# Two-layer encoder: output weights on the sync queue behind two activation loads, and eight constant matmuls at the start

## The chip, the cores and the metric

The kernel runs on one core of a Trainium2 chip. A core has a matrix engine (TensorE, "PE" in the profile, with its weight loads listed as "PEld"), a vector engine (VectorE, "DVE"), a scalar engine (ScalarE, "ACT"), a general engine (GpSimd, "POOL") and a sync engine ("SP") that only issues transfers. Each engine runs its own instructions in their order and waits on semaphores for the others. Transfers between the main memory (HBM) and the on-chip memory (SBUF) are done by 16 DMA engines; in this kernel they are issued from SP and from POOL. Matmul results land in PSUM banks, which DVE and ACT read.

The metric is the device time of one execution in microseconds (us). Lower is better.

## The reference

A trunk of two layers over 1024 frames of width 1024, in float32. Layer 0 mixes with multi-head latent attention, layer 1 with differential attention; each mixer is followed by a residual and a LayerNorm, then by a SwiGLU block with a residual and a LayerNorm. What matters here is the start (the first projection of `x`) and the output projection of layer 1:

```python
h = x @ w_in                                   # layer 0, first work of the kernel
...
# layer 1, differential attention, 8 heads of 128 values
a = p[:, 0] - lam * p[:, 1]
o = jnp.einsum('bhqk,bkhe->bqhe', a, v)
o = _rmsnorm(o, g_sub) * (1.0 - lambda_init)
mix = o.reshape(b, s, DIFF_HEADS * DIFF_V) @ w_o
h = _layernorm(ALPHA * h + mix, g, b)
```

## The kernel before

**Products in parts.** Float32 operands are split into a high part and a remainder ("h" and "l"), and a product is three matmuls: high by high, high by low, low by high. ACT makes the high part, DVE or POOL the remainder.

**The planner.** The program is written in one order, and a planner with a timeline model then places each instruction in its engine's queue. Instructions stay in the order that the data need, but an instruction may be moved ahead of others that it does not depend on. Which DMA goes to which queue is fixed by the line that issues it (`nc.sync` is SP, `nc.gpsimd` is POOL); the place in the queue is the planner's.

**The start.** `load_x` and `load_w_in` (lines 930 to 952) bring the first two token blocks of `x` in quarters and the eight slices of the input weights, split them, and `project` (line 969) multiplies them. Line 979 and line 980 are its matmuls, for columns 0 to 383 and 384 to 703. Before the first of them the matrix engine has nothing to do. The tile `ones` (all entries 1/128) is filled by `V.memset` on line 1033; it is later the stationary side of the RMS norm in layer 1.

**The attention of layer 1.** The function `attention` (line 258) runs over 64 blocks: eight heads by eight token blocks of 128 rows. Head 7 takes its token blocks in the order `LAST_ORDER` = 6, 7, 4, 5, 2, 3, 0, 1. For a block, `score_b` makes two score maps (matmuls of line 216 into three "s" banks, biased and reduced by DVE on line 219, exponentials by ACT on line 222, POOL on line 1281, DVE on line 1282), `turn_b` transposes them (line 148), and `mix_b` multiplies with the values (line 255). Scores are made two blocks ahead. A list of fillers (`at(slot, ...)`) puts other work between the blocks.

**The output projection of layer 1** (class `OutProj`, line 325) is spread over the attention of head 7. At slot 54 `begin_out` (line 1369) closes the pool of the transposed activations and makes the object. Its constructor loads the activations of the first token block (`of`, six heads, 128 rows each of 512 B: line 354) from `o_dr`, where the attention has put the finished heads; then the output weights of the eight heads, already split, from `wo_dr` (1 MB a head). Heads 0 to 5 go to tiles of the pool `op1` (line 341); heads 6 and 7 go in halves to tiles of the pool `wp` (line 346). All ten weight loads are issued from POOL. `of` also splits the block (ACT on line 377, DVE on line 378) and loads its residual rows (line 372). For the second token block `of` is called by a filler four slots later. `early` multiplies heads 0 to 5 of the first and second token block (line 389) while head 7 is still under way: heads 0 and 1 of the first block at slot 56, heads 2 and 3 at slot 57, 4 and 5 at slot 58, then the second block at slots 60 and 61. `late` adds heads 6 and 7, which stay on the chip, and `rest` does the other six token blocks. In `rest` POOL also loads the gain and bias of the LayerNorm (line 419).

Of the kernel before, what the change touches and what calls it, by code (L numbers as in the profile page):

```python
# [16 lines left out]
P = 128  # L17
# [21 lines left out]
LAST_ORDER = (6, 7, 4, 5, 2, 3, 0, 1)  # L39
# [3 lines left out]
def trunk(  # L43
# [32 lines left out]
    nc = tc.nc  # L76
    V, A, G, T = nc.vector, nc.scalar, nc.gpsimd, nc.tensor
# [5 lines left out]
    ones = cp.tile([P, P], F32, tag="ones", name="ones")  # L83
# [15 lines left out]
    banks("ps0", PS_BUFS_A)  # L99
    dr = ctx.enter_context(tc.tile_pool(name="dr", bufs=1, space=DRAM))  # L100

    mhalf = cst[:, 0:2]
    V.memset(mhalf, -0.5)
    eps_rms = cst[:, 8:9]
# [2 lines left out]
    def f32(t):  # L107
        return t.bitcast(F32)
# [4 lines left out]
    def ps_s(name):  # L113
        return ps.tile([P, 512], F32, tag="s", bufs=ps_bufs[0], name=name)

    def ps_m(name):
        return ps.tile([P, 512], F32, tag="m", bufs=ps_bufs[1], name=name)
# [3 lines left out]

    def ps_o(name):
        return ps.tile([P, 512], F32, tag="o", bufs=ps_bufs[3], name=name) if len(ps_bufs) > 3 else ps_m(name)

    def small(name, n=1):
        return sp.tile([P, 2], F32, tag="small", name=name, bufs=22)[:, :n]
# [119 lines left out]
    def pv_group(pts, g, v_of, name):  # L246
        po = ps_o(f"o_{name}")
        nj = 2 * g + 2
        for j in range(nj):
            hi, lo = pts[j // 2]  # L250
            vh, vl = v_of(j)
            c = slice(P, 256) if j == nj - 1 else slice(0, 256)
            first, last = j == 0, j == nj - 1
            for a, b, st, sp_ in ((vh, hi, first, False), (vh, lo, False, False), (vl, hi, False, last)):
                T.matmul(po[:, c], a, b[:, j % 2, c], start=st, stop=sp_, skip_group_check=True)
        return po
# [68 lines left out]
    class OutProj:  # L325
# [5 lines left out]
        def __init__(self, side, w_dr, o_dram, o_here, x_src, x_dst, scale):  # L331
            self.st = ExitStack()
            self.pool = self.st.enter_context(tc.tile_pool(name="op1", bufs=2, side=side, reuse_waits="tile"))
            self.o_dram, self.o_here, self.x_src, self.x_dst, self.scale = o_dram, o_here, x_src, x_dst, scale
            self.oh, self.z, self.sums, self.m = {}, {}, {}, {}
            self.of(LAST_ORDER[0])
            self.wo = []
            for h in range(H):
                if h < self.HEADS:
                    t = self.pool.tile([P, 2, D], F32R, tag=f"wo{h}", name=f"wo1_{h}", bufs=1)  # L340
                    nc.gpsimd.dma_start(t, w_dr[h])
                    self.wo.append((t[:, 0], t[:, 1]))
                else:
                    t = [wp.tile([P, D], F32R, tag=f"w{p}", name=f"w{p}o1_{h}") for p in "hl"]
                    for p in range(2):
                        nc.gpsimd.dma_start(t[p], w_dr[h][:, p])
                    self.wo.append(t)

        def of(self, tb):
# [136 lines left out]
    def ffn(side, xo, xst, pending, layer, x_src, x_dst, lng, lnb, next_x):  # L486
# [419 lines left out]
        st.close()  # L906
        return new, rest, normed

    o_dr = [[dr.tile([H, P, 256], F32, name=f"o_dr{l}_{g}") for g in range(4)] for l in range(2)]
    wo_dr = [dr.tile([P, 2, D], F32, name=f"wo_dr{h}") for h in range(H)]  # L910
    xs_dr = [dr.tile([S, D], F32, name=f"xs_dr{l}") for l in range(3)]
# [118 lines left out]

    gs = cst[:, 16:17]
    nlam = cst[:, 24:25]
    V.memset(ones, 1.0 / P)
    lv = [late[:, 64 * i:64 * i + 64] for i in range(4)]
    dots = late[:, 256:258]

# [14 lines left out]
    with ast as st:  # L1051
# [100 lines left out]
        def at(slot, fn, *args):  # L1152
            fill.setdefault(slot, []).append(lambda: fn(*args))
# [49 lines left out]
    with ExitStack() as st:  # L1203
# [162 lines left out]
        first, second = LAST_ORDER[:2]  # L1366
# [7 lines left out]
        at(b, begin_out)  # L1374
        for slot, what, args in (
            (2, "early", (first, (0, 1))), (3, "early", (first, (2, 3))), (4, "early", (first, (4, 5))),
            (4, "of", (second,)), (6, "early", (second, (0, 1, 2))), (7, "early", (second, (3, 4, 5))),
            (9, "late", (first,)),
        ):
            at(b + slot, lambda what, *a: getattr(proj[0], what)(*a), what, *args)  # L1380
# [97 lines left out]
```

## Time and profile before

| | |
|---|---|
| median of 3 runs | 2318.11 us (2317.43 to 2320.41) |
| the profiled execution | 2317.24 us, of which its span is 2315.5 us |
| granted matrix clock over the span, mean | 0.992 |
| busy: PE, DVE, ACT, POOL | 2253.4, 1560.1, 1018.5, 891.9 us |
| DMA | 288.29 MB, 125 GB/s on average |

The span runs from the first to the last instruction of the profiled execution; the rest of its time lies around that. The matrix engine is busy for nearly all of the span, so the other engines' times matter only where the matrix engine waits for them. Busy shares are averages over stages with different limits; what an edit is worth is read at its own place.

### The profile page before, as it was taken

To read this page: it belongs to the slowest core of one execution; us is meant where nothing else is said; L and a number is where in the kernel's file an instruction comes from. 1 tells how busy PE (TensorE), PEld (TensorE's weight loads), DVE (VectorE), ACT (ScalarE), POOL (GpSimd) and SP (SyncE) were. 2 spreads that over 40 slices of the span, in tenths; PEclk is the share of its full clock that TensorE was granted. 3 is DMA by queue.
4 is the path that set the end of the run, shared out by engine and by line. 5 is a ranking of instruction groups with operands and counts; after the bars stand their busy time and mean duration, and the time that the engine had idled before them with its cause. 6 is when DMAs were issued, how large, how long until landed. Compare 5 with 4: busy or idle time off the path is not lost. (4 is left out here: it accounts for less than half of the span.)

```text
span 2315.5 us, 31126 instructions
## 1 busy us (share of the span) xinstructions
PE 2253.4 (97%) x11410; PEld 1918.7 (83%) x11410; DVE 1560.1 (67%) x2879; ACT 1018.5 (44%) x2092; POOL 891.9 (39%) x698
## 2 busy tenths in 40 slices
PE   9999999999999999999999999979999999999997
PEld 9898897888888887888888898967778888887886
DVE  5666664596666658677476766666596656658777
ACT  4466673352332324345465656545442333324343
POOL 2233351014444445465332423222014444436564
PEclk9999999999999999999999999989999999999999
DMA  5121335334323238454310202153344222337453
GB/s 202 41 91 69 106 101 178 125 142 145 125 76 129 86 119 322 182 183 140 101 46 31 71 25 69 37 191 111 126 144 149 99 103 102 113 129 303 146 203 121
DMA packets 103658, 288.29 MB, mean 125 GB/s; under 512 B 8528, under 2 KB 31696, under 8 KB 93008
## 3 DMA queue, kind: packets, MB, share of 16 engines
q1 hardware_dynamic: 98064, 268.46, 33.0%
q0 software_dynamic: 5440, 17.83, 2.3%
q8 instruction: 90, 1.47, 0.3%
q14 instruction: 64, 0.52, 0.1%
HBM read 205.00 MB, written 77.07 MB: 122 GB/s over the span
## 5 line engine op out<-in xcount | busy, mean ns | idle before, releaser
L469 ACT CAST op_g<-gr 128x512 fp32r<-128x512 f32 x240 | 147.5, 622 | 411.0 <-PE gb L514 228.3
L470 POOL TENSOR_TENSOR op_g<-gr,op_g 128x512 fp32r<-128x512 f32 x104 | 145.8, 1407 | 303.6 <-DVE tmp L605 153.6
L470 DVE TENSOR_TENSOR op_h<-rh,op_h 128x512 fp32r<-128x512 f32 x154 | 162.8, 1088 | 67.6 <-ACT op_h L469 67.6
L514 PE MATMUL ga<-xh_m,op_g 128*128 128x512 f32 x512 | 168.0, 389 | 0.0
L469 ACT CAST op_h<-rh 128x512 fp32r<-128x512 f32 x154 | 93.0, 619 | 145.0 <-PE dx L782 37.5
L782 PE MATMUL dw<-op_w_t,op_h 128*128 128x512 f32 x660 | 151.4, 390 | 0.0
L782 PEld LDWEIGHTS dw<-op_w_t,op_h 128*128 128x128 f32 x660 | 123.6, 188 | 25.9 <-DVE op_h L470 0.4
L222 ACT ACTIVATE l_b<-l_b,mx_b 128x256 f32<-128x256 f32 (+7 forms) x128 | 99.6, 778 | 76.2 <-DVE mx_b L219 74.2
L1281 POOL TENSOR_SCALAR l_b<-l_b,r_b,cst 128x128 f32<-128x128 f32 (+3 forms) x64 | 52.8, 825 | 205.1 <-DVE r_b L224 196.1
L470 POOL TENSOR_TENSOR op_w_t<-tt,op_w_t 128x512 fp32r<-128x512 f32 x66 | 98.8, 1501 | 77.1 <-ACT op_w_t L469 77.1
L782 PE MATMUL dx<-op_w_b,op_h 128*128 128x512 f32 x528 | 122.7, 392 | 5.9 <-ACT op_w_b L469 3.9
L782 PEld LDWEIGHTS dx<-op_w_b,op_h 128*128 128x128 f32 x528 | 98.3, 188 | 29.9 <-ACT op_w_b L469 4.7
L514 PE MATMUL gb<-t4h_f,op_g 128*128 128x512 f32 x352 | 115.8, 390 | 3.0 <-DVE tmp L597 3.0
L514 PE MATMUL gc<-b22h_f,op_g 128*128 128x512 f32 x352 | 115.6, 389 | 1.6 <-ACT op_g L469 1.6
L470 DVE TENSOR_TENSOR op_g<-gr,op_g 128x512 fp32r<-128x512 f32 x136 | 109.5, 807 | 9.0 <-ACT op_g L469 8.8
L514 PE MATMUL gc<-t1h_f,op_g 128*128 128x512 f32 x352 | 115.5, 389 | 0.0
L514 PE MATMUL gb<-t3h_f,op_g 128*128 128x512 f32 x352 | 115.2, 389 | 0.0
L514 PE MATMUL gb<-t2h_f,op_g 128*128 128x512 f32 x352 | 114.8, 389 | 0.0
L514 PEld LDWEIGHTS ga<-xh_m,op_g 128*128 128x128 f32 x512 | 96.1, 188 | 19.9
L470 POOL TENSOR_TENSOR op_g<-s,op_g 128x512 fp32r<-128x512 f32 x40 | 55.3, 1382 | 143.6 <-ACT op_g L469 143.6
L143 PE MATMUL bp<-xT_f,h_wb 128*128 128x512 f32 x256 | 103.4, 404 | 0.0
L145 PE MATMUL bp<-xT_f,l_wb 128*128 128x512 f32 x256 | 101.8, 398 | 0.0
(375 smaller groups left out, 6788.4 us busy)
## 6 DMA issues: line engine op xcount, KB each, us to landing
gr<-in_w_gu SPq DMA_DIRECT2D x44, 1024.0 KB, 6.7
rh<-h_dr SPq DMA_DIRECT2D x28, 1024.0 KB, 5.3
h_dr<-sh SPq DMA_DIRECT2D x22, 1024.0 KB, 4.9
h_dr<-hp SPq DMA_DIRECT2D x22, 768.0 KB, 4.1
tt<-in_w_dn SPq DMA_DIRECT2D x22, 512.0 KB, 7.5
rh<-h_dr SPq DMA_DIRECT2D x14, 768.0 KB, 4.3
z<-xs_dr SPq DMA_DIRECT2D x16, 512.0 KB, 10.0
rw_b<-in_w_dn SPq DMA_DIRECT2D x8, 1024.0 KB, 8.7
```

Source lines behind the costliest of these rows:

```text
L143: T.matmul(ps_out, lh, rh, start=(i == 0), stop=False)
L145: T.matmul(ps_out, ll, rh, start=False, stop=(i == n - 1))
L222: A.activation(l[:, :n], l[:, :n], AF.Exp, bias=mx, scale=-1.0, accum_out=sm)
L469: A.copy(hi, src)
L470: eng.tensor_tensor(lo, src, f32(hi), ALU.subtract)
L514: T.matmul(o, w[:, a, kc], x[b][:, k, :], start=(first and k == 0 and (a, b) == (0, 0)), stop=(k == 3 and a == 1), skip_group_check=True,)
L782: T.matmul(o, h[:, a, c], w[:, b_], start=(first and (a, b_) == (0, 0)), stop=(last and a == 1), skip_group_check=True,)
L1281: G.tensor_scalar(l1[:, :n], l1[:, :n], r1, nlam, ALU.mult, ALU.mult)
```

## The change

Two edits. The first concerns the output projection of layer 1: the constructor of `OutProj` now calls `of` for both first token blocks before the weights (the filler that called it for the second is taken out), and the ten weight loads are issued from SP instead of POOL. As the tiles hold the type `float32r` and the source is float32, the destination is written as float32 through a view (`f32(t)`); the bytes are the same.

The second adds a function `spin` that issues `n` matmuls of the constant tile `ones` with itself into one "s" bank that nothing reads, and calls it with eight of them before the first loads are written; the `V.memset` of `ones` is moved to the head of the program for that.

```diff
+    V.memset(ones, 1.0 / P)
     mhalf = cst[:, 0:2]
...
+    def spin(n, name):
+        t = ps_s(name)
+        for i in range(n):
+            T.matmul(t[:, :P], ones, ones, start=True, stop=True)
...
-            self.of(LAST_ORDER[0])
+            for tb in LAST_ORDER[:2]:
+                self.of(tb)
...
                     t = self.pool.tile([P, 2, D], F32R, tag=f"wo{h}", name=f"wo1_{h}", bufs=1)
-                    nc.gpsimd.dma_start(t, w_dr[h])
+                    nc.sync.dma_start(f32(t), w_dr[h])
...
                     for p in range(2):
-                        nc.gpsimd.dma_start(t[p], w_dr[h][:, p])
+                        nc.sync.dma_start(f32(t[p]), w_dr[h][:, p])
...
+    spin(8, "spin0")
+
     o_dr = [[dr.tile([H, P, 256], F32, name=f"o_dr{l}_{g}") for g in range(4)] for l in range(2)]
...
-    V.memset(ones, 1.0 / P)
...
-            (4, "of", (second,)), (6, "early", (second, (0, 1, 2))), (7, "early", (second, (3, 4, 5))),
+            (6, "early", (second, (0, 1, 2))), (7, "early", (second, (3, 4, 5))),
```

## The prediction

> **What bounds the kernel now.** I read the page first (its head and part 1), then the list of what each engine waited for, kept to the matrix engine over the whole span.
>
> ```profile
> span 2315.5 us, 31126 instructions
> PE 2253.4 (97%) x11410; PEld 1918.7 (83%) x11410; DVE 1560.1 (67%) x2879; ACT 1018.5 (44%) x2092; POOL 891.9 (39%) x698
> ...
> PE s_b L216 <- DVE mx_b L219: 14.3, 1, 14.3
> PE hq L979 <- ACT wih L950: 4.3, 1, 4.3
> ```
>
> PE is idle for 2315.5 - 2253.4 = 62.1 us in all. The two longest single waits are the places that the change touches: 14.3 us in one piece at line 216 (scores of head 7), and 4.3 us before the first matmul. PE sets the end and a hole in PE is worth its length if PE then runs on without a new one. Next, busy time by stretches around the first hole (after the time: busy us of PE, PEld, DVE, ACT, POOL, then the granted clock, DMA share, GB/s), and the timeline of PE.
>
> ```profile
> 1500.00:1520.00 20.00, 19.18 (x111) 16.38 (x110) 14.13 (x34) 9.57 (x18) 5.99 (x11) 1.00 0.27 97
> 1520.00:1540.00 20.00, 5.70 (x17) 4.25 (x17) 5.08 (x17) 4.01 (x8) 4.45 (x6) 0.68 1.08 402
> ...
> 1519.83 0.71 PE L389 MATMUL zp_a<-wo,oh_a 128*128 128x512 f32 x2 [0.37 <-DMA wo<-wo_dr]
> ...
> 1536.21 0.79 PE L216 MATMUL s_b<-bk,bq 128*128 128x512 f32 x1 [14.30 <-DVE mx_b L219]
> ...
> 1537.22 1.05 PE L389 MATMUL zp_a<-wo,oh_a 128*128 128x512 f32 x2
> ...
> 1540.64 0.48 PE L216 MATMUL s_b<-bk,bq 128*128 128x512 f32 x1
> 1540.96 0.39 PE L216 MATMUL s_b<-bk,ql 128*128 128x512 f32 x1
> 1541.19 0.62 PE L389 MATMUL zp_a<-wo,oh_a 128*128 128x512 f32 x2
> ```
>
> All four compute engines are nearly still from 1520 to 1540 while DMA is full (402 GB/s against 97 before). And the hole costs twice: after it the clock is low. The ten 512-column matmuls from 1536.21 to 1540.64 take 4.43 us, 0.44 each; from 1540.96 to 1541.19 one takes 0.23. At 0.23 the ten would take 2.3, so 2.1 us are lost there. Who holds DVE? ACT, which holds itself for a transfer:
>
> ```profile
> 1533.76 1.02 DVE L378 SCALAR_TENSOR_TENSOR oh_a<-of_a,cst,oh_a 128x768 fp32r<-128x768 f32 x1 [13.50 <-ACT oh_a L377]
> ...
> 1517.18 0.94 ACT L377 ACTIVATE oh_a<-of_a,cst 128x768 fp32r<-128x768 f32 x1
> 1532.79 0.93 ACT L377 ACTIVATE oh_a<-of_a,cst 128x768 fp32r<-128x768 f32 x1 [14.67 <-DMA of_a<-o_dr]
> ...
> 1513.55 0.96 SPq L354 DMA_DIRECT2D of_a<-o_dr  x2
> 1519.68 15.47 SPq L354 DMA_DIRECT2D of_a<-o_dr  x2
> ...
> 1513.82 3.25 POOL L341 DMA_DIRECT2D wo<-wo_dr  x6 [3.76 <-PE bp L145]
> 1517.07 0.54 POOL L419 DMA_DIRECT2D gb<-in_ln_mix_g  x1
> 1519.98 0.54 POOL L346 DMA_DIRECT2D who<-wo_dr  x1 [1.85 <-DMA wo<-wo_dr]
> ...
> 1528.21 0.54 POOL L346 DMA_DIRECT2D wlo<-wo_dr  x1 [2.14 <-DMA wo<-wo_dr]
> ...
> of_a<-o_dr SPq DMA_DIRECT2D x8, 384.0 KB, 4.6
> ...
> gb<-in_ln_mix_g POOLq DMA_DIRECT2D x1, 512.0 KB, 17.8
> ```
>
> SP issues both activation loads at 1513.55 (0.48 apart, two in 0.96). The first is used at 1517.18, 3.6 us later. The second was issued at 1514.03 and is used only at 1532.79, 18.8 us later, although a load of this kind lands in 4.6 us in the median. Between, POOL put 6 MB of weights and 1 MB of gains on the same engines. The small rows of the second load had to share with them almost to their end. So the hole is not work, it is one 384 KB transfer behind a bulk that nobody needs yet.
>
> **The change part by part.** *Second activation load ahead of the weights on one queue.* It is issued at 1514.03 as before. Its landing is bounded below by the 3.6 us of the first (1517.6), and above by the median 4.6 plus one gain load's worth of sharing, 2.7 us (below), so 1521.3. ACT is free at 1518.1 (1517.18 + 0.94): its stall of 14.67 becomes 0 to 3.2 us. From ACT's start to PE's restart took 1536.21 - 1532.79 = 3.4 us, so scores could go on at 1521.0 to 1524.7.
>
> *What is late next: the weights.* POOL's last four issues each waited for the landing of one of heads 0 to 3: from 1519.98 to 1528.21 that is three steps, 2.74 us for 1 MB. Head 0 landed about 6.0 us after its issue (PE waited for it until 1519.83; issue 1513.82). In the new order it is third on SP: issued at 1514.5, and up to 2 us behind the two activation loads (0.75 MB at 2.74 us a MB). I take 1521.7 (ends 1520.5 and 1522.5). Then heads 1 to 5 land at 1524.4, 1527.2, 1529.9, 1532.7, 1535.4. POOL has nothing ahead of its two gain loads now (1 MB, quoted at 1517.07), and they may share from the start: everything up to 2.7 us later. I count that delay in full.
>
> PE takes the heads in a fixed order with scores between. From where each head starts I read how much PE work stands until 1553.07, where head 5 of the first block is done:
>
> ```profile
> 1544.12 0.62 PE L389 MATMUL zp_a<-wo,oh_a 128*128 128x512 f32 x2
> ...
> 1548.68 0.63 PE L389 MATMUL zp_a<-wo,oh_a 128*128 128x512 f32 x2
> ...
> 1551.68 0.63 PE L389 MATMUL zp_a<-wo,oh_a 128*128 128x512 f32 x2
> ...
> 1553.07 0.60 PE L148 MATMUL pt_b<-ident,l_b 128*128 128x128 f32 x4
> ```
>
> Heads 1, 2, 3, 4 and 5 start at 1537.22, 1541.19, 1544.12, 1548.68 and 1551.68. At full clock the work left is 14.3 us from head 1 (1553.07 - 1537.22 less about 1.6 of the low clock), 11.9, 9.0, 4.4 and 1.4. PE is through at the latest of landing plus work left: 1538.7, 1539.1, 1538.9, 1537.1, 1536.8; head 2 decides, 1539.1. That is 14.0 us before 1553.07; with the gain loads in front 1541.8, or **11.3 us**. With no wait on weights at all the gain would be the hole and the slow stretch, 14.3 + 2.1 = 16.4, which is the upper end. Lower end: the same chain with PE at the low clock through half its 14 us, 7 us more, leaves 4.3. I take 11.3.
>
> *The ten weight loads leave POOL for SP.* SP issues ten more, about 0.48 us each, 4.8 us in all; behind them there stand the third and fourth activation loads (quoted at 1519.68) and the residual rows. Those activations are used at 1574.38:
>
> ```profile
> 1574.38 1.75 ACT L377 ACTIVATE oh_a<-of_a,cst 128x768 fp32r<-128x768 f32 x2
> 1574.54 0.48 PE L389 MATMUL zp_a<-who,oh_a 128*128 128x512 f32 x1
> ```
>
> Cover of over 30 us even if the whole 8 MB go first (8 x 2.74 = 22 us after 1514.5), so nothing is counted. Heads 6 and 7 are first used at 1574.54, about 1563 in the new time; they land by 1541 to 1544. On POOL, line 1281 stood behind the weight loads; it now goes earlier, also not counted, as DVE was the one that waited. The view as float32 adds no instruction.
>
> *Eight constant matmuls.* At the start:
>
> ```profile
> 0.89 0.17 DVE L1033 MEMSET ones<- 128x128 f32 x1
> 4.25 0.69 PE L979 MATMUL hq<-wih,xh 128*128 128x384 f32 x1 [4.25 <-ACT wih L950]
> 5.73 0.63 PE L980 MATMUL hk<-wih,xh 128*128 128x320 f32 x1 [0.79 <-ACT wih L950]
> ...
> 11.17 0.47 PE L980 MATMUL hk<-wih,xl 128*128 128x320 f32 x1
> ...
> 12.03 0.31 PE L980 MATMUL hk<-wih,xl 128*128 128x320 f32 x1
> ...
> 31.52 0.82 PE L148 MATMUL cp<-ident,cn 128*128 128x128 f32 x6
> ```
>
> The planner had put the memset at 0.89 already, so moving it is worth nothing. The eight can start at 1.06. The nearest price is the six 128-column transposes, 0.82 together, about 0.14 each at full clock, 0.28 at half: 2.2 us, done by 3.3. At twice that they end at 5.5, still in the wait for the second half of the first weights (5.73). So their cost is nothing up to 0.3 us. The gain: a 320-column matmul takes 0.47 still at 11.17 and 0.31 at 12.03, the low clock and the full one. If the full rate came at 5.73, the 5.4 us up to 11.17 would hold at most 2.7 us less; operands that arrive late take some of it back. If the eight, with the gaps that follow them, don't bring the clock up sooner, it is 0. The profile's granted clock can't tell: it shows 1.00 in this stretch. I take 1.0.
>
> The row after the big hole says the clock needed 4.4 us of unbroken matmuls there. The Trainium skill ("TensorE: Matmul & The Clock Gate", Part 1) says the full clock comes after about 3.4 us of busy time, in a window that runs free of the kernel's start. By that rule the gain would be anywhere between 0 and 2.7 by chance of phase; the sum here stands without it.
>
> *Sum.* Profiled execution 2317.24 (span 2315.5 and 1.7 around it) less 11.3 less 1.0 = **2304.9 us**. The median of the runs shown is 0.9 higher.
>
> **The rivals.** (1) *The transfers interleave whatever queue they come from*, so the second load still lands late; the hole stays and only the start can move: 2317.2 less 0 to 2.7, or 2314.5 to 2317.2. For it: the 18.8 us above. Against it: on one queue, loads issued one after the other land in that order:
>
> ```profile
> 12.52 0.43 SPq L967 DMA_DIRECT2D kt<-in_c_krope  x1
> 13.47 0.57 SPq L1022 DMA_DIRECT2D cos<-in_c_cos  x1
> ...
> kt<-in_c_krope SPq DMA_DIRECT2D x1, 512.0 KB, 6.0
> cos<-in_c_cos SPq DMA_DIRECT2D x1, 512.0 KB, 7.6
> ```
>
> That is 18.5 and 21.1. The Trainium skill ("DMA: Bandwidth & Descriptors", "Issuing engines are not separate DMA queues") says that transfers of all issuing engines run on the same 16 and interleave, which would give this rival; its section "Queues, rings and completion order" has one queue's descriptors taken in order, which the two loads agree with. 8%.
>
> (2) *The planner puts the weights in front.* The tiles of the later heads lie where activations were that become free before the last of them; the planner moves loads that are ready. Every weight head ahead of the second activation load delays it by 2.74 us. With k heads in front it lands at 1514.0 + 3.6 + 2.74k; the old 1532.8 is reached at k = 5.5. With all eight in front it is 1539.5, **6.7 us slower than before**: 2317.2 + 6.7 less 1.0 = 2323. From six on there is no gain. Against it: the first loads on SP (1513.55) and POOL (1513.82) go at the same moment, and POOL's row names a matmul of line 145 as its releaser, the last that reads the old activations. 7%.
>
> (3) *Paced by weights at a low clock.* PE idles in short pieces while it waits for heads, the clock drops again, and half the work runs at half rate: 4.3 instead of 11.3, 2312. 15%.
>
> (4) *No gain loads in front, and the clock up early:* 14.0 to 16.4 and 2.7, or 2298 to 2300.5. 12%.
>
> **How the numbers follow.** The forecast (2301 to 2309) has 58%, rival (3) 15%, (4) 12%, (1) 8%, (2) 7%. A measurement of this kernel can tell about 0.2%, 4.6 us, from no change; faster means below 2313.5. Rivals (3) and (4) and the forecast lie below it, less 2% for a (3) that comes out dearer: 0.83 faster. Same: (1) and that 2%, 0.10. Slower: (2), 0.07. The range 2299 to 2314 takes in the forecast, nearly all of (3) and most of (4), about 8 in 10.
>
> **What would show it.** Right: the ACT wait at line 377 below 4 us, the 14.3 us wait of PE at line 216 gone, and new waits of PE at line 389 for weight loads of some 2 us each. The second activation load lands within 8 us of its issue, and head 5 of the first block ends 9 to 14 us earlier against the start of the loads. At the start, 320-column matmuls of 0.31 before 11 us. Wrong: the ACT wait stays above 10 us, SP rows with weights ahead of line 354, or new PE waits elsewhere in the span, which would mean that the planner has reordered more than this.

## The result and the profile after

| | median us | runs | lowest to highest |
|---|---|---|---|
| before | 2319.26 | 4 | 2317.43 to 2321.85 |
| after | 2306.58 | 4 | 2304.65 to 2308.88 |

The ratio is 0.9945, 95% interval 0.9932 to 0.9958: 12.7 us less. The profiled execution of the changed kernel was the slowest of its four, 2308.88 us with a span of 2306.8.

In the changed kernel and in all experiments the lines are numbered 8 to 10 higher: the load of activations is line 363, its split 386 (ACT) and 387 (DVE), the weight loads 350 and 355, the output matmul 398, scores 224 and 227, the gain load 428, the constant matmuls 131. The head of the page and part 1, two of the longest waits of PE, and busy time by stretches (us of PE, PEld, DVE, ACT, POOL, then granted clock, DMA share, GB/s), all of the changed kernel:

```profile
span 2306.8 us, 31138 instructions
PE 2257.6 (98%) x11426; PEld 1924.4 (83%) x11426; DVE 1560.0 (68%) x2879; ACT 1017.6 (44%) x2092; POOL 883.7 (38%) x688
```

```profile
PE dx L791 <- ACT op_w_b L478: 3.9, 2, 2.0
...
PE zp_a L398 <- DMA wo<-wo_dr: 3.3, 1, 3.3
```

```profile
1500.00:1520.00 20.00, 18.04 (x106) 15.37 (x104) 14.72 (x35) 11.16 (x21) 3.43 (x4) 1.00 0.31 110
1520.00:1540.00 20.00, 18.18 (x101) 15.80 (x102) 14.18 (x43) 9.40 (x22) 2.29 (x2) 0.91 1.01 412
```

PE's idle time is 2306.8 - 2257.6 = 49.2 us, against 62.1 before. The 14.3 us wait at the scores and the 4.3 us wait at the start are gone from the list. From 1520 to 1540 DMA is as full as before (412 GB/s), but PE works for 18.18 of the 20 us, where it had 5.70. The bulk transfer is the same; only what waits behind it is not. The granted clock is not back to full, though: it is 0.91 in this stretch, and behind the new 3.3 us wait the first six 512-column matmuls, from 1521.82 to 1524.51, take 0.45 us each where 0.23 is the full rate. The order of issue on SP, the split on ACT, the first output matmuls on PE and the gain load on POOL (timelines of the changed kernel):

```profile
1512.59 0.96 SPq L363 DMA_DIRECT2D of_a<-o_dr  x2
1513.60 2.90 SPq L350 DMA_DIRECT2D wo<-wo_dr  x6
1516.55 1.00 SPq L355 DMA_DIRECT2D who<-wo_dr  x2
1521.70 3.81 SPq L355 DMA_DIRECT2D wlo<-wo_dr  x2
```

```profile
1516.21 1.94 ACT L386 ACTIVATE oh_a<-of_a,cst 128x768 fp32r<-128x768 f32 x2
```

```profile
1521.82 2.05 PE L398 MATMUL zp_a<-wo,oh_a 128*128 128x512 f32 x4 [3.33 <-DMA wo<-wo_dr]
...
1541.73 0.39 PE L398 MATMUL zp_a<-wo,ol_a 128*128 128x512 f32 x1
```

```profile
1513.44 0.59 POOL L428 DMA_DIRECT2D gb<-in_ln_mix_g  x1 [4.34 <-PE s_b L224]
```

Both loads go first on SP. ACT does both splits in one piece (x2) without a wait between them. PE waits 3.3 us once, for head 0 of the weights, and head 5 of the first block is done at about 1541.9, where before it was 1553.1. Counted from the issue of the first activation load this is 29.4 us against 39.5, or 10.2 us earlier.

**Where the time went.** One execution can be laid over another by the start times of the DVE instructions that both have; the median difference in the stretch that begins at the time given, in us, against the profiled execution of before (a calculation from the two timelines; four of the experiments below stand beside the change, as they are used later):

```
from (us)        100     400    1000    1300    1560    1700
after           -1.2    -3.9    -3.8    -1.0   -12.2    -8.6
e1               0.4     0.4     0.7    -0.5   -10.7    -9.9
e4               0.8    -1.6    -1.2    -2.4    -1.8    -1.6
e6              -1.1    -1.5    -1.3    -2.5   -14.6   -15.4
e11             -1.8    -2.9    -2.8    -2.6   -11.8    -8.2
```

The step at the output weights is 11.2 us (from -1.0 to -12.2); the end of head 5 gave 10.2. Steps of 2 to 3 us come and go elsewhere, and they must be read with care: e4, whose order on every engine is that of before, shows some too. A part of what is lost again after 1560 is taken up in the last section.

### The profile page after: what moved, and what is told of

Read it like the earlier page. It is cut to its first block, busy times and chain, and to the rows that moved or that the text cites. A ratio compares the mean times of both kernels' runs of the same rounds, so it can differ in the third digit from the quotient of the medians.

```text
span 2306.8 us, 31138 instructions
## 1 busy us (share of the span) xinstructions
PE 2257.6 (98%) x11426; PEld 1924.4 (83%) x11426; DVE 1560.0 (68%) x2879; ACT 1017.6 (44%) x2092; POOL 883.7 (38%) x688
```

## The experiments

All were timed beside the kernel before, whose medians in the three sets were 2320.21 (21 runs), 2320.04 (11) and 2319.84 (27).

| kernel | weights issued from | constant matmuls | median us | ratio, 95% interval |
|---|---|---|---|---|
| e1 change without constant matmuls | SP | 0 | 2309.62 | 0.9953, 0.9940 to 0.9966 |
| e2 constant matmuls alone | POOL | 8 | 2316.18 | 0.9984, 0.9974 to 0.9993 |
| e3 queue alone | SP | 0 | 2307.32 | 0.9943, 0.9930 to 0.9957 |
| e4 earlier call alone | POOL | 0 | 2319.81 | 1.0001, 0.9988 to 1.0015 |
| e5 split placed late | POOL | 0 | 2310.60 | 0.9957, 0.9945 to 0.9969 |
| e6 weights held | POOL | 0 | 2303.73 | 0.9931, 0.9917 to 0.9944 |
| e7 change, gains behind | SP | 8 | 2304.24 | 0.9930, 0.9918 to 0.9942 |
| e8 queue alone, gains behind | SP | 8 | 2303.32 | 0.9927, 0.9915 to 0.9939 |
| e9 five constant matmuls | POOL | 5 | 2317.09 | 0.9987, 0.9978 to 0.9996 |
| e10 twelve constant matmuls | POOL | 12 | 2316.94 | 0.9990, 0.9981 to 0.9999 |
| e11 held, constant matmuls | POOL | 8 | 2308.66 | 0.9949, 0.9936 to 0.9963 |
| e12 held, constant matmuls, gains held | POOL | 8 | 2313.29 | 0.9974, 0.9965 to 0.9983 |

### The parts of the change

The change taken apart. The theory at this point was the prediction's: the 7 MB must stand behind the second load. The rivals were that the sync queue is worth it by itself, or the earlier call.

**e1: the change without the constant matmuls.**

```diff
-    V.memset(ones, 1.0 / P)
...
-    spin(8, "spin0")
```

> The change without the eight constant matmuls: both activation loads first and the weights on SP. Main theory (the second load gets its bytes ahead of the weights, and that is nearly all of the gain): 10 to 11.5 us faster than the kernel before, ACT's wait at the split of the second block below 1 us, first weight head used about 3 us after PE is ready for it. Rival (the start is worth more than 1 us by what the planner makes of it): less than 9 us faster.

2309.62, or 10.6 us less than before: the two loads ahead of the weights make nearly all of the gain. PE waited 3.6 us for the first weights.

**e2: the constant matmuls alone.** The kernel before with `spin(8, "spin0")` and the early memset.

> Only the eight constant matmuls; the output projection as before. Main theory: 0 to 2 us faster, the start of layer 0 about 1.2 us earlier as in the trace of the changed kernel, the 14 us wait of PE in head 7 unchanged. Rival (the planner's other order is worth several us): 3 us or more either way.

2316.18, or 4.0 us less (interval 1.6 to 6). The main theory gave 0 to 2 and missed; the value lies in the rival's range. The hole of 14.3 us is there as before. The size is taken up again with e9 and e10.

**e3: the queue alone.** The ten weight loads from SP, with `of` for the second block back in the filler at its old slot.

```diff
-            for tb in LAST_ORDER[:2]:
+            for tb in LAST_ORDER[:1]:
                 self.of(tb)
...
-            (6, "early", (second, (0, 1, 2))), (7, "early", (second, (3, 4, 5))),
+            (4, "of", (second,)), (6, "early", (second, (0, 1, 2))), (7, "early", (second, (3, 4, 5))),
```

> Weights on SP, but the second activation load called where it was before; no constant matmuls. The planner's SP queue then has six whole weight loads and two halves, 7 MB, between the two activation loads. Main theory (order on the one queue decides): the second load lands at about 3.6 + 7 x 2.74 = 22.8 us after the first is issued, 4 us later than in the kernel before, so 2 to 5 us slower than before. Rival (what counts is that POOL is rid of the weight loads): about 10 us faster.

This fell. The planner did put 7 MB ahead of the second load, and the load was as late as ever, yet the kernel was 12.9 us faster than before. SP's and ACT's timelines, and the tile view of that one load's landing (min, median, max from issue):

```profile
1514.47 0.37 SPq L363 DMA_DIRECT2D of_a<-o_dr  x1
1514.89 2.91 SPq L350 DMA_DIRECT2D wo<-wo_dr  x6
1517.84 0.92 SPq L355 DMA_DIRECT2D who<-wo_dr  x2
1520.88 0.37 SPq L363 DMA_DIRECT2D of_a<-o_dr  x1
```

```profile
1541.15 0.95 ACT L386 ACTIVATE oh_a<-of_a,cst 128x768 fp32r<-128x768 f32 x1
```

```profile
DMA to landing us min/median/max: 19.6/19.6/19.6
```

Issued at 1520.88, landed 19.6 us later at 1540.5, later than in before. But the split of the second block doesn't stand where it stood. With everything on one queue the planner placed the split at 1541.15, behind the exponentials of three more blocks, as if it knew that the load comes late. The split waited for nothing; PE waited 2.4 us in two pieces for weights.

**e4: the earlier call alone**, with the weights still on POOL.

> Only the earlier call of the second activation load; weights on POOL, no constant matmuls. The planned order is the same as before on all five engines, only the tiles lie elsewhere. Main theory: no difference, within 1.5 us; ACT waits 14 us again. Rival (the earlier call is what brings the gain): 10 us faster.

2319.81, no difference; ACT's wait is 15.4 us and PE's 15.2. The planner's order on all five engines is that of before.

### What decides: the bytes or the place of the waiting instruction

After e3 there were three theories. A: what cost was one ACT instruction (and the DVE one behind it) that waited for late data in front of others on an engine that runs in order. B: the order of the bytes. C: the sync queue itself.

**e5: the split moves.** The kernel before with one line of ordering: the split stands behind the exponential where e3 had it. The planner placed other instructions anew behind it, but until 1543 us on the clock of before PE's order is that of before, so the hole is met with the same work on PE.

```diff
+    exps = []
...
-        A.activation(l[:, :n], l[:, :n], AF.Exp, bias=mx, scale=-1.0, accum_out=sm)
+        exps.append(A.activation(l[:, :n], l[:, :n], AF.Exp, bias=mx, scale=-1.0, accum_out=sm).ins)
...
-            A.activation(oh, o, AF.Copy, scale=self.scale)
+            x = A.activation(oh, o, AF.Copy, scale=self.scale)
+            tb == LAST_ORDER[1] and not hs.start and behind(x.ins, exps[-5])
```

> The kernel before with one thing added: the split of the second block's activations is held on ScalarE behind the second 128x640 exponential of the last head, where it stood in the kernel with the queue alone changed (there it began at 1541.15 us). Weights on GpSimd's queue, second load at its old place, no constant matmuls. Theory A (what cost was that an instruction waiting for late data stood ahead of others on an engine that runs in order; where the bytes stand doesn't matter): the load still lands 15 to 20 us after its issue, but ScalarE's 14.67 us wait and TensorE's 14.3 us wait go; a wait of 2 to 5 us for the first weights takes their place; 8 to 11 us less than before. Theory B (the order of the bytes decides: the second load has to be ahead of the 7 MB): the load is as late as before and its wait only moves; within 3 us of before. Theory C (the sync queue itself is worth it): within 2 us of before.

2310.60, or 9.4 us less. ACT's timeline, the landings of the first two loads, and PE's wait for weights in the stretch from 1500 to 1580:

```profile
1514.99 0.94 ACT L386 ACTIVATE oh_a<-of_a,cst 128x768 fp32r<-128x768 f32 x1
...
1538.06 0.92 ACT L386 ACTIVATE oh_a<-of_a,cst 128x768 fp32r<-128x768 f32 x1
```

```profile
DMA to landing us min/median/max: 3.5/11.9/20.2
```

```profile
PE zp_a L398 <- DMA wo<-wo_dr: 0.5, 1, 0.5
```

The same queues, the same bytes, the second load 20.2 us under way (18.8 before), and the hole is gone. B and C fall as conditions: with neither, most of the gain is there. One instruction some 17 places too early in ACT's queue was the cause of the whole 14.3 us wait. 9.4 us of it were gained, as PE then waits elsewhere in the stretch, in pieces of 2.5 us and less.

**e6: the bytes in order, on POOL.** Both loads first; each weight transfer, still from POOL, behind a small POOL write that reads the second activation tile (`raw` keeps it). The half loads of heads 6 and 7 have such a write in front of them too.

```diff
-                    nc.gpsimd.dma_start(t, w_dr[h])
+                    G.tensor_scalar(t[:, 0, 0:1], self.raw[LAST_ORDER[1]][:, 0, 0:1], 1.0, None, ALU.mult)
+                    nc.gpsimd.dma_start(t, w_dr[h])
```

> The kernel before with the second load issued directly behind the first, and each weight tile's transfer, still on GpSimd's queue, behind a one-column GpSimd write to it that reads the second activation tile (the transfer overwrites that column, so what is computed is the same). So the weights' bytes can't start before the second load has landed. No constant matmuls. Theory A (an instruction that waits in order for late data) and theory B (order of the bytes) both expect the 14.67 us wait of ScalarE to fall under 4 us, and the first weights later than in the changed kernel by the landing of the load (3 to 4 us) and ten small GpSimd operations: a wait of 4 to 9 us for them on TensorE; 4 to 9 us less than before. Theory C (the sync queue itself is worth it): within 2 us of before.

2303.73, or 16.3 us less: more than either theory gave (4 to 9), and without constant matmuls. POOL issues the first weight transfer at 1518.99, 8.0 us after the first activation load, where SP did so 1.0 us after it in the changed kernel. Yet PE waits less for it, not the expected 4 to 9 us:

```profile
1518.99 0.60 POOL L350 DMA_DIRECT2D wo<-wo_dr  x1
```

```profile
PE s_b L224 <- DVE mx_b L227: 2.1, 1, 2.1
PE zp_a L398 <- DMA wo<-wo_dr: 1.1, 1, 1.1
```

The wait on the load is now one that the planner sees, so it placed PE's output matmuls later and other work before them (1.1 us of wait where the change has 3.3). That is A once more, on PE: what counts is that the place of an instruction in its queue fits the arrival of its data. From 1500 to 1600 PE waits 3.8 us in all, against 6.1 in the changed kernel, and the step at the output weights is 12.1 us in the timelines laid over each other (from -2.5 to -14.6), against 11.2. That leaves some 4 of the 16.3 us without a shown place, and most of the 5.9 us between e6 and e1 as well.

### The gain loads

**e7: the change with the gain loads behind the weights.**

```diff
-                nc.gpsimd.dma_start(gb[:, i], src.partition_broadcast(P))
+                nc.sync.dma_start(gb[:, i], src.partition_broadcast(P))
```

> The changed kernel with the two gain loads (1 MB written) issued from the sync queue, behind the weights, in place of GpSimd's queue, where they ran ahead of them. The prediction's term (these bytes stand ahead of the first weights and cost 2.7 us): the first weights land 2 to 3 us earlier, TensorE's 3.3 us wait for them falls to 0.3 to 1.3, and the time is 2 to 3 us under the changed kernel's 2306.6, so 2303.5 to 2304.6 (13.5 to 16.5 us under before). The rival (the weights' own bytes pace TensorE over the six heads, so that an earlier first head is lost at the second or third): waits of 1 us or more appear at a later head, and the time is within 1 us of 2306.6.

2304.24, which is 2.3 us under the changed kernel, as expected; the two intervals overlap. Not as expected is the place: the first wait only fell from 3.3 to 2.7 us, where 0.3 to 1.3 had been expected. The landings of the six whole heads from their own issue (min is head 0, max is head 5), first in the changed kernel, then in e7:

```profile
DMA to landing us min/median/max: 8.1/14.3/20.2
```

```profile
DMA to landing us min/median/max: 7.4/12.3/17.5
```

Without the gain loads head 0 lands 0.7 us sooner and head 5 2.7 us sooner. So the 1 MB did cost 2.7 us over six heads, but the gain bytes did not stand ahead of the weights, they shared with them. PE waits for head 0 alone in both kernels, so its waits show only 0.7 us of this; whether the rest of the 2.3 us comes from the gain loads isn't shown.

The Trainium skill ("DMA: Bandwidth & Descriptors", "Issuing engines are not separate DMA queues") has transfers of different issuing engines interleave on the same 16 engines; these numbers agree.

**e8: the queue alone, with constant matmuls and the gains behind.** e3 with these two.

> The kernel with the queue alone changed (second load left at its old place, which the planner sets behind 7 MB of weights), with the eight constant matmuls and the gain loads behind the weights. If the parts add up (12.9 us for the queue alone, 1 to 4 for the constant matmuls, 0 to 1.5 for the gain loads, since the wait for the first weights was only 0.63 there): 13.5 to 17 us under before, 2302 to 2306, so no slower than the changed kernel though the second load's bytes come later than in any other version. If the early second load is needed after all (the queue-only result was luck in the planner's order): 2309 or more.

2303.32, or 16.7 us less, as the sum of the parts gave. PE's waits from 1500 to 1560, all of them, and the stretch by busy time:

```profile
PE o_b L263 <- ACT pth_b L251: 0.5, 1, 0.5
PE s_b L224 <- DVE bk L1277: 0.4, 1, 0.4
PE zp_a L398 <- ACT oh_a L386: 0.4, 1, 0.4
PE zp_a L398 <- DVE ol_a L387: 0.2, 1, 0.2
```

```profile
1520.00:1540.00 20.00, 19.32 (x113) 16.45 (x112) 16.59 (x48) 10.96 (x25) 2.31 (x2) 1.00 1.02 410
```

PE waits for no weights at all, and the clock stays at 1.00 while 410 GB/s come in. The second load is 17.4 us under way and nobody notices. This version and e6 are the fastest measured, about 3 us under the changed kernel; their intervals and that of the change just overlap.

### The constant matmuls

Eight of them gained 4.0 us alone, where the prediction had 1.0. They also change the planner's order (some 160 rows on PE). Five leave that order as it was, twelve nearly so.

**e9: five**, `spin(5, "spin0")` in the kernel before.

> The kernel before with five constant matmuls at the start in place of eight, nothing else. With five the planner leaves every engine in the order of before (with eight it changed the order of some 160 of 8,700 TensorE rows). At 0.47 us each they last 2.4 us, so the first real matmul waits for nothing new. If what eight of them gained alone (4 us, interval 2 to 6) came from the clock of the first microseconds: 0.5 to 2 us less than before, and all medians against before between -0.5 and -2 from 20 us on, with no step later. If it came from the planner's order: within 1 us of before, and in the trace the same steps as before or those that the kernels without constant matmuls show.

**e10: twelve**, `spin(12, "spin0")`.

> The kernel before with twelve constant matmuls, nothing else. The planner's order is again nearly that of before (21 TensorE rows differ). They last until about 6.7 us at 0.47 us each, or less if the clock rises within them. If the clock of the start is worth something beyond the prediction's 1.0: full clock from the first real matmul, which starts 0 to 2 us later than in before; between 0.5 us more and 2.5 us less than before. If the gain of eight was the planner's order: within 1 us of before.

2317.09 and 2316.94, or 2.8 and 2.9 us less. Both lie outside both cases of their expectations. With five the order on every engine is that of before, so a new order isn't needed for the gain. The start of PE in e9, in the change and in e10:

```profile
1.04 2.50 PE L131 MATMUL spin<-ones 128*128 128x128 f32 x10 [1.04 <-DVE cst L106]
...
7.77 0.47 PE L991 MATMUL hk<-wil,xh 128*128 128x320 f32 x1
...
8.27 0.31 PE L991 MATMUL hk<-wih,xl 128*128 128x320 f32 x1
```

```profile
1.04 3.78 PE L131 MATMUL spin<-ones 128*128 128x128 f32 x16 [1.04 <-DVE cst L106]
...
4.95 0.47 PE L991 MATMUL hk<-wih,xh 128*128 128x320 f32 x1
...
7.08 0.31 PE L991 MATMUL hk<-wih,xh 128*128 128x320 f32 x1
```

```profile
1.05 4.66 PE L131 MATMUL spin<-ones 128*128 128x128 f32 x24 [1.05 <-DVE cst L106]
...
5.72 0.30 PE L991 MATMUL hk<-wih,xh 128*128 128x320 f32 x1
```

(Each constant matmul is two rows.) Full clock, read from the 320-column matmuls (0.31, low 0.47), comes at 8.3, by 7.1 and by 5.7 us, and at 11.7 before. In the timelines laid over before, the six kernels with eight constant matmuls are 0.9 to 1.8 us ahead from 60 to 100 us (1.4 in the mean), the one with twelve 1.3, and the one with five 0.1 behind; the five others, without any, lie between 1.1 ahead and 0.7 behind. By 345 us five of the seven with eight or twelve have lost 1.0 to 1.6 us of this again. So the start is worth no more than about what the prediction gave it, 1.0, and the medians say about 3.

Most of the rest shows at one place much later. At some 355 us, just behind the wait of 2.7 us on line 255 or 263 that the last section comes back to, PE begins the output projection of layer 0. In before (first row) it waits there once more, for a copy by ACT; in e9 (second row) it doesn't, although the order is the same:

```profile
358.35 0.80 PE L143 MATMUL zp_a<-wo,oh_a 128*128 128x512 f32 x1 [0.73 <-ACT ob L1147]
```

```profile
357.63 0.73 PE L151 MATMUL zp_a<-wo,oh_a 128*128 128x512 f32 x1
```

The wait is there in all six profiled kernels without constant matmuls and in none of the eight with them. From the end of the 2.7 us wait to the start of the twelfth of these matmuls it takes 9.0 to 9.5 us in five of the six (7.1 in e4) and 6.1 to 7.4 us in the eight, so the clock is back sooner there. All eight step 2.2 to 3.3 us ahead of before between 345 and 400 us: e9 and e10 by 2.3 each, of the 2.8 and 2.9 in their medians. Why ACT's copy no longer holds PE isn't shown: the matmul doesn't read what is copied, and no run varies this alone. The clock alone can also make the step, as in e4, which has the wait and steps by 2.4 us. And the single profiled executions don't keep it: those of e2, e9 and e10 end 0.6 to 1.9 us behind that of before, with steps back at other places, where their medians over many runs are ahead. So that this place makes the medians is likely, and not proved.

### The held version with the constant matmuls

**e11: e6 with the eight; e12: that with the gain loads held as well.**

```diff
+    spin(8, "spin0")
...
+                G.tensor_scalar(gb[:, i, 0:1], self.raw[LAST_ORDER[1]][:, 0, 0:1], 1.0, None, ALU.mult)
                 nc.gpsimd.dma_start(gb[:, i], src.partition_broadcast(P))
```

> The kernel with the weights held on GpSimd's queue until the second load has landed (2303.73, 16.3 us under before), with the eight constant matmuls of the change. If these are worth 3 to 4 us whatever stands beside them: 2299 to 2301. If they are worth the prediction's 1.0: 2302 to 2303.5. If the planner's order around the output weights was what made the held version fast, and the new order takes it back: 2305 or more.

> The same, with the two gain loads held behind the second load as well and issued behind the first six weights. Their bytes (1 MB) then stand behind the first weights, which land about 2.6 us earlier. If TensorE still waits for weights there (1.1 us in the held version): 0 to 1.5 us under the version without this edit. If the planner has other work in that place, which the held version's 1.1 us wait speaks for: within 1 us of it.

2308.66 and 2313.29: 4.9 and 9.6 us slower than e6. e11's number is that of the third case of its expectation, but the reason given there, a new order around the output weights, isn't what its trace shows: up to the first output weights the order is that of e6. The first weight transfer is issued at 1518.97 (1518.99 in e6) and lands 7.7 us later, where e6's took 5.2, and DMA moves 321 to 345 GB/s from 1520 to 1526, where it moved 379 to 425. So PE waits 3.4 us for the first weights where e6 waited 1.1. The step at the output weights is 9.2 us (12.1 in e6), and 3.6 us of it are lost again by 1700. Why the transfer was slower, and whether it is in every execution, stays open; the intervals of e6 and e11 just overlap. e12 misses both cases of its expectation, with 4.6 us more than e11. A part of what e12 lost is in sight: POOL, DVE and PE in order of time.

```profile
1532.25 0.53 POOL L355 DMA_DIRECT2D wlo<-wo_dr  x1 [2.82 <-DMA wo<-wo_dr]
1534.92 0.53 POOL L355 DMA_DIRECT2D wlo<-wo_dr  x1 [2.14 <-DMA wo<-wo_dr]
1535.49 2.26 POOL L1291 TENSOR_SCALAR l_b<-l_b,r_b,cst 128x896 f32<-128x896 f32 x2
```

```profile
1536.62 2.08 DVE L1292 SCALAR_TENSOR_TENSOR l_b<-l_b,r_b,l_b 128x896 f32<-128x896 f32 x1 [3.05 <-POOL l_b L1291]
```

```profile
1538.85 1.73 PE L156 MATMUL pt_b<-ident,l_b 128*128 128x128 f32 x7 [3.56 <-DVE r_b L232]
```

POOL's last issues wait until earlier transfers have landed. Two more transfers on POOL bring the next real POOL instruction, line 1291, to 1535.49 (1530.55 in e11, 1528.79 in e6), and DVE and PE stand behind it; PE's wait is 3.56 us. What else e12 lost isn't placed. It is the fault of before on a third engine: an instruction that waits for a transfer in front of one that doesn't need it. Here it is the issue of a DMA that waits, and on SP, which only issues, the same wait costs nothing (e7 and e8).

## Why the prediction was right, and where its reasons were not

It gave 2304.9 (2299 to 2314), faster; measured 2306.58. Predicted was 12.3 us less than the profiled execution of before; between the two medians it is 12.7.

- **The hole** of 14.3 us: gone, as said. The low clock behind it is not: the new wait of 3.3 us brought it back for six matmuls, some 1.3 us. **ACT's stall** of 0 to 3.2: 0. The second load landed 4.2 us after its issue in the changed kernel, within the bounds of 3.6 and 7.3. Of the signs that it named, only the waits for weights came otherwise: one of 3.3 us, not several of some 2.
- **The weights next**: sized 11.3, and 10.2 to 11.2 in the timelines, 10.6 in e1. That it came out so close is in part luck, since two errors go against each other. Head 0 landed 1.8 us before the time that the sum counted with (1524.4 with the gain loads in front, 1522.6 measured on the clock of before). But from there to the end of head 5 PE took 20.1 us, where the prediction's rows give about 16.7 (1.9 for head 0 and the scores behind it, 0.5 for the scores at 1536.21 at full clock, and the 14.3 from head 1 on): the clock was low at first, and the planner put other work between. The step that was to decide, the landing of head 2, did not: it landed at 1527.63 and was first used at 1531.13.
- **The gain loads**: counted in full as 2.7 us in front of everything. e7 shows 0.7 at head 0 and 2.7 at head 5, by sharing, and only the 0.7 is seen in PE's waits.
- **The reason was too narrow.** The prediction held the place of the split for given and concluded that the bulk has to come behind the second load. Its rival (2), the planner putting the weights in front, came true in e3 with seven of the eight heads in front. For seven its rule gives a landing at 1536.8 and a time 4.0 us slower than before. The load landed at 1540.5, later still, and the kernel was 12.9 us faster: the rule was wrong by 16.9 us, because the planner moved the instruction as well as the load. e5 shows the cause by itself: the order of instructions on ACT is enough (9.4 us). The change works because either of its halves brings the place of the split and the arrival together: data first, or (one queue) an order in which the split comes late.
- **POOL to SP at no cost**: held; e12 shows what issuing from POOL can cost when transfers pile up there.
- **The constant matmuls**: 1.0 at the start agrees with the profiles (about 1.4 with eight), but the medians of e2, e9 and e10 say 2.8 to 4.0, with intervals from about 0.2 to 6. The prediction had nothing for the place at 355 us, where the profiles of all eight kernels with them gain 2.2 to 3.3 us; why they gain there isn't settled. e11's profile has both gains, and its median is nevertheless 4.9 us above that of e6, as more was lost at the output weights and behind them.
- **Rival (1)**, interleaving whatever the queue, is true between queues (gain loads, 2.7 us by head 5) and not within SP's: in e3 the second load, issued behind seven heads, landed at 1540.45, behind the last of them (1539.36).

## What to carry to other kernels

When an engine shows one long wait for a transfer, look first at what stands behind the waiting instruction: moving that one instruction (e5, 9.4 us) was worth nearly as much as moving 8 MB of transfers (e1, 10.6). Give the planner a truth that it can see, by one queue or a real dependence, since two queues that it takes for independent share the same DMA engines. If bulk is issued from an engine that also computes, look at what stands behind the issues: POOL was held up in e12, though in e6, also on POOL, it cost nothing that shows. And compare versions by medians of many runs, since two edits that seem to have nothing to do with each other need not add up: the constant matmuls, a gain of some 3 us beside before, came with a loss of 4.9 beside the held weights (e11), and the cause isn't known.

## What the runs showed of the hardware that was not expected

**The same short wait costs the clock in one execution and not in another.** In the SwiGLU block of layer 1 PE waits for a split of line 478 in both the changed kernel and e6:

```profile
1682.15 0.79 PE L523 MATMUL gc<-b22h_f,op_g 128*128 128x512 f32 x1 [2.61 <-ACT op_g L478]
...
1685.24 0.63 PE L523 MATMUL ga<-xh_m,op_gp 128*128 128x512 f32 x2
```

```profile
1676.68 0.50 PE L523 MATMUL gc<-b22h_f,op_g 128*128 128x512 f32 x1 [2.56 <-ACT op_g L478]
...
1677.25 0.42 PE L523 MATMUL ga<-xh_m,op_gp 128*128 128x512 f32 x1
...
1677.74 0.62 PE L523 MATMUL ga<-xh_m,op_gp 128*128 128x512 f32 x2
```

After 2.61 us idle the changed kernel's next seven matmuls take 3.09 us, 0.44 each; after 2.56 us e6's next four take 1.06, 0.27 each. That is 1.5 us, and a part of the 3.6 that the changed kernel's profiled execution lost again after 1560. The same can account for a part of the scatter between executions, though how much isn't shown: before and e4 have one and the same order, and around a wait of 2.7 us on line 255 (263 in e4), with one of about 1.7 just ahead of it, their clock differs (first before, then e4):

```profile
355.00:360.00 5.00, 4.26 (x17) 3.79 (x17) 1.23 (x1) 2.83 (x5) 0.72 (x1) 0.50 0.92 349
360.00:365.00 5.00, 5.00 (x17) 3.94 (x16) 0.00 (x0) 0.00 (x0) 1.79 (x2) 0.68 0.98 307
```

```profile
355.00:360.00 5.00, 4.26 (x22) 3.93 (x22) 1.56 (x3) 2.04 (x4) 0.00 (x0) 0.72 0.98 382
360.00:365.00 5.00, 5.00 (x24) 4.11 (x23) 0.26 (x1) 0.79 (x2) 2.54 (x2) 1.00 0.94 278
```

PE is busy for the same 9.26 us in both, and does 46 matmuls in one and 34 in the other. e4, 0.8 us behind before in the timelines until there, is 1.6 us ahead just behind it. The Trainium skill ("TensorE: Matmul & The Clock Gate", Part 1) describes a window of about 3.4 us that runs free of the kernel; that the outcome differs at equal order agrees with it, but here waits of 2.6 us were enough to lose the clock, less than the idle window that it names.
